# A chunked recurrence on one core: the two halves of a chunk taken one after the other, with four gaps for dense matmuls in place of three

## The chip, the cores and the metric

The kernel runs on one core of one Trainium2 chip. The metric is the device time of one execution in microseconds (us). PE is TensorE, PEld its weight loads, DVE VectorE, ACT ScalarE, POOL GpSimd, SP SyncE; DMAs are issued on SP's queue.

## The reference, cut to what matters

One layer runs (DEPTH is 1): RWKV-7 time mixing over 2048 tokens, 16 heads of 64 channels, width 1024. Projections give r, k, v, a gate and a decay for every token; then a state of 64x64 for each head is carried from token to token, and its output is normed by head, given a bonus, gated and projected out:

```python
def step(S, inp):
    r_t, w_t, k_t, v_t, kk_t, a_t = inp
    sa = jnp.einsum('bhvk,bhk->bhv', S, -kk_t)
    S = (S * w_t[:, :, None, :] + sa[..., None] * (kk_t * a_t)[:, :, None, :]
         + v_t[..., None] * k_t[:, :, None, :])
    return S, jnp.einsum('bhvk,bhk->bhv', S, r_t)
...
y = (y - mean) * lax.rsqrt(var + RW_GN_EPS)
y = y * gn_w + gn_b
y = y + jnp.sum(r_h * k_h * r_k, axis=-1, keepdims=True) * v_h
return (y * g) @ w_out          # and the layer adds x
```

## The kernel before, in words

**Stages.** The first stage projects v, the gate and the low-rank inputs for all tokens. The second makes k, r and, for every chunk of 32 tokens, the small matrices of the recurrence; its last part (function `last`, four steps for each of eight head groups) runs together with chunks 0 to 8. The third stage is the loop over chunks 9 to 63 with `chunk(ch, after)`. The change lies in `chunk` and in what goes with it, so in chunks 0 to 8, in the loop and in what follows it.

**A chunk.** 32 tokens, 16 heads. A chunk has two halves, w = 0 and w = 1, of four pairs of heads each. The work of one half, by the names of the code:

- `s_mm` (L255): 8 fp32 matmuls, into the bank `ybank` number w; each fp32 matmul is two instructions in the trace. `s_out` (L261): two ACT copies of 32x256.
- `u_mm` (L267): 8 matmuls of what `s_out` wrote, into `ubank`. `u_out` (L273): two ACT copies into `x`, the operand of the chunk.
- `y_mm` (L279): 8 matmuls, the chunk's output, into `ybank` number w. `y_out` (L290, L292): ACT copies to `y`, in every second chunk.
- `d_mm` (L300): 16 matmuls, the state, into the other half of the bank `ubank`. `d_out` (a DVE multiply, recorded at the helper's line L52 as x<-ubank,misc): two of 64x256 into the `x` of the next chunk.

Each matmul writes one strip of 32 of PE's columns. `s_mm`, `u_mm` and `y_mm` of a half use two of the four strips, `col(h, ch)` or `col(h, ch + w)`, which for neighbouring chunks are the other two; `d_mm` goes round all four.

**The order of the work.** All engines run their instructions in the order in which the code issues them. `chunk` issues three groups, each followed by a call `fill(i)`: `s_mm` of (ch, 0) interleaved with `u_mm` of (ch-1, 1); `u_mm` of (ch, 0) interleaved with `y_mm` of (ch-1, 1), then `d_mm` of (ch-1, 1); `d_mm` of (ch, 0), then `s_mm` of (ch, 1) interleaved with `y_mm` of (ch, 0). `finish` completes the last half. In the loop a `fill` is `after(i)`, which calls two planners:

- `background(us)` issues entries of the queues `evacs` (stores of the output) and `work`, each with a price in us written in the code, up to a budget; `served[1]` keeps what is left, but never more than one call's budget. An entry (None, None) ends a call, unless it is the first thing that the call meets. The first entry of a call is issued whatever its price.
- `fill(n)` issues about n output matmuls (L500) from the queue `dense`: 0.7 n when 36 or fewer wait (`LOW`), n when more, 1.3 n when over 72.

```python
served[1] = min(served[1] + us, us)
fresh = True
while evacs or work:
    u, fn = (evacs or work)[0]
    if not fresh and (u is None or u > served[1]):
        break
```

**The tail of 128 rows.** After chunks 12, 16, ..., 60, `work` gets `tail(t)`, the norm, bonus, gate and transposes of four finished chunks: squares on ACT, four sums and two seeds on DVE, three Newton steps on POOL, then five DVE operations for each of four parts, two groups of four transposes on PE (L460), a copy (L480) and a subtraction each; at its end 48 dense matmuls enter `dense`, whose two results make four `store` entries. After chunks 12, 16, ..., 40 up to ten entries of the inversion of the last two blocks' matrices follow (60 columns in all, two DVE operations each, price 0.5). `y` has three buffers: `more_y(t)` calls `background(1)` until the transposes of tail t-3 have been issued. When the loop is over, `tail(15)` is queued, and `background(2)` and `fill(6)` alternate until all queues are empty.

Of the kernel before, what the change touches and what calls it, by code (L numbers as in the profile page):

```python
# [10 lines left out]
I32 = mybir.dt.int32  # L11
# [12 lines left out]
NP = 8  # L24
# [1 line left out]
TB = 256  # L26
NC = TB // L
NORM_EPS = 1e-6
F, BG, EV, EV0, GWE, BNE, LOW, SLOW, FAST, INV, INVC = 4, (1.5, 1.3, 3.2), (0, 0, 0), (0, 0, 0), 0, 0, 36, 0.7, 1.3, (8, 10), 0.5
LIM = 1.0  # L30
TURN = 1e-9
INL = (0, 0, 3, 3, 3, 0, 0, 0)
# [8 lines left out]
def rwkv7_kernel(ctx, tc, a, T):  # L41
    nc = tc.nc
# [270 lines left out]
    def chunk(ch, fill):  # L313

        g, c = divmod(ch, NC)
        go = ch != first[0]
        if c == 2 and g + 1 < NB:
            load_g(g + 1)
        for p in range(4):
            s_mm(ch, 0, p)  # L320
            if go:
                u_mm(ch - 1, 1, p)
        s_out(ch, 0)
        if go:
            u_out(ch - 1, 1)
        fill(0)
        for p in range(4):
            u_mm(ch, 0, p)
            if go:
                y_mm(ch - 1, 1, p)  # L330
        if go:
            d_mm(ch - 1, 1)
        u_out(ch, 0)
        if go:
            y_out(ch - 1, 1)
            d_out(ch - 1, 1)
        if ch + 2 < NCH:
            load_v(ch + 2)
        if ch + 3 < NCH:
            load_c(ch + 3)  # L340
        fill(1)
        d_mm(ch, 0)
        for p in range(4):
            s_mm(ch, 1, p)
            y_mm(ch, 0, p)
        d_out(ch, 0)
        s_out(ch, 1)
        y_out(ch, 0)
        fill(2)

    def finish(ch):
        for p in range(4):
            u_mm(ch, 1, p)
        u_out(ch, 1)
        for p in range(4):
            y_mm(ch, 1, p)
        d_mm(ch, 1)
        d_out(ch, 1)
        y_out(ch, 1)

    dense, evacs, turned, served, al = deque(), deque(), set(), [0.0, 0.0], {}
    eng = lambda i: nc.gpsimd if i else nc.vector

    def fill(n):

        served[0] = min(served[0], 6) + n * (FAST if len(dense) > 2 * LOW else 1 if len(dense) > LOW else SLOW)
        while served[0] > 0 and dense:
            dense.popleft()[0]()
            served[0] -= 1
# [2 lines left out]
        while any(x[1] == key for x in dense):  # L372
            dense.popleft()[0]()

    def tail(t):

        y = ys.pop(t)
        b, q = t // 2, t % 2
        orow = slice(t * P, (t + 1) * P)
        bc = lambda z: z[:, :, None].broadcast_to([P, z.shape[1], N])  # L380
        bn = bns[b][:, 2 * q : 2 * q + 2]
        st, out = {}, []
        part = lambda c: (slice(None), c // 2, slice(4 * (c % 2), 4 * (c % 2) + 4))

        def step(us):
            return lambda fn: out.append((us, fn))

        def sml(nm):
            return al["sml"](f"{nm}{t}")

        def load_bonus(k):
            st["v", k] = v = al["v"](f"v{t}_{k}")
# [11 lines left out]
        @step(0.1)  # L404
        def _():
            st["var"], st["rst"] = sml("var"), sml("rst")
            load_bonus(0)
            load_bonus(1)
            square(0)
            square(1)  # L410

        for c in range(4):
            @step(0.4)
            def _(c=c):
                nc.vector.tensor_reduce(st["var"][part(c)], st["sq", c], AX.X, add)
                if c < 2:
                    square(c + 2)

        rs_tt = lambda o, x, y: al["rs"].tensor_tensor(out=o, in0=x, in1=y, op=mul)
# [1 line left out]

        @step(0.4)
        def _():
            var = st["var"]
            st["rg"], st["rm"] = sml("g"), sml("m")
            ts(var, var, 1.0 / N, GN_EPS, mul, add)
            ts(st["rg"].bitcast(I32), var.bitcast(I32), -0.5, 1597463007.0, mul, add)
            rs_ts(var, var, -0.5, mul)

        for it in range(3):  # L430
            @step(al["newton"])
            def _(it=it):
                var, g, m = st["var"], st["rg"], st["rm"]
                rs_tt(m, g, g)
                rs_tt(m, m, var)
                rs_ts(m, m, 1.5, add)
                rs_tt(g if it < 2 else st["rst"], m, g)

        for k in range(2):
            out.append((0.1, lambda k=k: scale_bonus(k)))  # L440
        out.extend([(None, None), (0.6, lambda: None)] * al["wait"])

# [64 lines left out]
            stt(x, st[n][:, q * 256 : q * 256 + 256], 0.5, x, mul, add)  # L507
            nc.sync.dma_start(a["out"][orow, o : o + 256], x)

        out.append((0.0, lambda: (load_gate(0), load_gate(1))))  # L510
        for k in range(2):
            for c in (2 * k, 2 * k + 1):
                out.append((0.7, lambda c=c: norm(c)))
                out.append((0.4, lambda c=c: bonus(c)))
                out.append((0.4, lambda c=c: shift(c)))
                out.append((0.4, lambda c=c: gating(c)))
            if k == 0:
                cut = len(out)
            if t == 0:

                out.append((TURN, lambda k=k: (transpose(k), high(k), rest(k))))
            else:
                out.extend([(None, None), (0, lambda k=k: (transpose(k), high(k))), (0.7, lambda k=k: rest(k))])
# [22 lines left out]
    with ExitStack() as p0:  # L546
# [152 lines left out]
        with ExitStack() as pb:  # L699
# [385 lines left out]
            with tc.manual_schedule(engines=MANUAL):  # L1085
# [107 lines left out]
                def fill_last(i):  # L1193
                    next(steps)
                    us = 0
                    while early:
                        if early[0][0] is None:
                            early.popleft()
                            if us:
                                break  # L1200
                        elif us + early[0][0] > LIM or early[0][0] is TURN and i != 2:

                            break
                        else:
                            us += early[0][0]
                            early.popleft()[1]()
                    if i == 2:
                        fill_last(3)

                steps = last()  # L1210
                for p in range(NP + 1):
                    chunk(p, fill_last)
                    if p == NP // 2:
# [6 lines left out]
                finish(NP)  # L1220
                while early:
                    fn = early.popleft()[1]
                    if fn:
# [2 lines left out]
    with ExitStack() as p1:  # L1226
# [44 lines left out]
        with tc.manual_schedule(engines=MANUAL):  # L1271
            work.extend((0.7, lambda q=q: wo_split(NP - 1, q)) for q in range(2))
            for x in tail(1):
                work.extend(x)
            z = c1.tile([P, L, L], F32, name="z_")
            tm = c1.tile([P, 4 * N], F32, name="tm_")
            inv = deque()
            for g in (NB - 2, NB - 1):
                load, *cols = inversion(g, z, lambda: tm)
                inv.extend([(0, load)] + [(None, None), (0, lambda: None)] * 4)  # L1280
                inv.extend((INVC, x) for x in cols)
            inv_g = inv[L + 6][1]

            inv_last = inv[-1][1]

            def after(i):
                background(BG[i])
                fill(F)

            for ch in range(NC + 1, NCH):  # L1290
                chunk(ch, after)
                if ch % 4 == 0 and ch > NC:
                    for x in tail(ch // 4 - 1):
                        work.extend(x)
                    for i in range(INV[1] if ch >= INV[0] else 0):
                        if inv:
                            work.append(inv.popleft())
                if ch == NCH - 2 * NC - 4:
                    assert len(inv) <= L - 1 and not any(x[1] is inv_g for x in work)
                if ch == NCH - NC - 4:  # L1300
                    assert not inv and not any(x[1] is inv_last for x in work)
            finish(NCH - 1)
            for x in tail(NCH // 4 - 1):
                work.extend(x)
            while work or dense or evacs:
                background(2)
                fill(6)
# [53 lines left out]
```

## Time and profile before

| | |
|---|---|
| time, median of 3 runs | 1640.67 us (1639.98 to 1648.12) |
| the profiled execution | 1649.95 us, its span 1648.1 us |
| busy in the span | PE 88%, PEld 72%, DVE 72%, ACT 46%, POOL 22% |
| chain that ended last | PE 50%, DVE 21%, ACT 9%, issue 6%, DMA 6% |
| mean granted TensorE clock | 0.972 |

The span goes from the first to the last instruction; 1.85 us of the profiled execution lie outside it. "Busy" counts a matmul until its modelled end, so a busy PE can still have gaps between its instructions. The shares are means over stages of different kinds; the chunk loop takes some 460 of the 1648 us.

### The profile page before, as it was taken

What the parts mean: (1) busy time and instruction counts of PE and PEld (TensorE: products, weight loads), DVE (VectorE), ACT (ScalarE), POOL (GpSimd) and SP (SyncE); (2) the same over time, 40 slices, a digit from 0 to 9 for tenths busy, and PEclk for the clock granted to TensorE, in tenths of its full rate; (3) what the DMA queues carried; (4) which work ended last, traced back from release to release, by engine and by line L of the source; (5) the groups of instructions that cost most, each with busy time, mean ns of one, the idle gap of its engine ahead of it and who ended that gap; (6) DMA issues with size and microseconds to landing.
All of it is one profiled execution on the core that took longest, in us unless ns stands there. A gap on an engine that the chain in (4) does not pass through costs nothing.

```text
span 1648.1 us, 48238 instructions
## 1 busy us (share of the span) xinstructions
PE 1442.2 (88%) x19024; PEld 1188.9 (72%) x19024; DVE 1187.9 (72%) x2876; ACT 762.3 (46%) x1908; POOL 358.8 (22%) x729
## 2 busy tenths in 40 slices
PE   3799999999989999999999998877777887787888
PEld 2578888888878888988888897765555555565556
DVE  7977687676835678888797978775567756785654
ACT  5653232233455545454545554665444444454440
POOL 4600000000002223232323223222222223222311
PEclk9899999999999999999999999998999999999999
DMA  5783333345563555666667677888555675566632
GB/s 180 231 260 138 129 134 122 112 144 167 197 192 84 154 114 147 133 162 154 157 163 152 163 154 189 220 239 210 162 164 175 174 185 173 163 183 184 194 114 74
DMA packets 413410, 269.79 MB, mean 164 GB/s; under 512 B 270048, under 2 KB 345440, under 8 KB 413184
## 3 DMA queue, kind: packets, MB, share of 16 engines
q1 hardware_dynamic: 411840, 262.19, 57.1%
q10 hardware_dynamic: 1344, 4.52, 1.2%
q8 instruction: 150, 2.46, 0.7%
q14 instruction: 76, 0.62, 0.1%
HBM read 159.26 MB, written 111.54 MB: 164 GB/s over the span
## 4 chain that ended last, share of the span: by engine, by line
PE 50%; DVE 21%; ACT 9%; issue 6%; DMA 6%; POOL 1%; SPq 1%; DVEq 0%; ACTq 0%; POOLq 0%
PE gps L582 9%; PE vps L582 8%; PE kps L582 7%; PE rps L890 5%; PE ops L500 4%; ACT x L273 4%; DVE x L52 3%; DVE y L52 3%; PE ubank L300 3%; PE lps L644 2%; PE ubank L267 2%; DVE z L52 2%; DVE tm L52 2%; PE mps L926 2%; ACT misc L261 2%
## 5 line engine op out<-in xcount | busy, mean ns | idle before, releaser
L52 DVE TENSOR_TENSOR x<-ubank,misc 64x256 f32<-64x256 f32 x216 | 91.2, 422 | 116.8 <-ACT x L273 100.2
L582 PE MATMUL kps<-mixbl,wkh 128*128 128x256 f32 x448 | 130.4, 291 | 15.2 <-DVE mixbl L187 15.2
L223 POOL MEMSET x<- 32x512 f32 x128 | 66.4, 519 | 329.1 <-PE ubank L300 249.8
L582 PE MATMUL kps<-mixbh,wkh 128*128 128x256 f32 x448 | 134.1, 299 | 0.2 <-DVE u L49 0.2
L890 PE MATMUL rps<-mixah,wrh 128*128 128x256 f32 x448 | 132.3, 295 | 2.1 <-ACT sq L61 2.1
L582 PE MATMUL kps<-mixbh,wkl 128*128 128x256 f32 x448 | 129.4, 289 | 0.0
L890 PE MATMUL rps<-mixal,wrh 128*128 128x256 f32 x448 | 126.5, 282 | 0.0
L890 PE MATMUL rps<-mixah,wrl 128*128 128x256 f32 x448 | 126.5, 282 | 0.0
L273 ACT COPY x<-ubank 32x256 f32<-32x256 f32 x220 | 79.9, 363 | 78.5 <-PE ubank L300 65.4
L500 PE MATMUL ops<-wol,oh 128*128 128x512 f32 x256 | 109.2, 426 | 1.8 <-issue 1.8
L500 PE MATMUL ops<-woh,oh 128*128 128x512 f32 x256 | 109.7, 429 | 0.4 <-DVE ol L52 0.4
L500 PE MATMUL ops<-woh,ol 128*128 128x512 f32 x256 | 109.7, 429 | 0.0
L300 PE MATMUL ubank<-x,dk 128*32 128x64 f32 x3456 | 72.7, 225 | 41.4 <-DVE x L52 18.6
L582 PE MATMUL vps<-wvh,mixah 128*128 128x512 f32 x256 | 104.0, 408 | 5.1 <-ACT mixah L97 4.7
L61 ACT ACTIVATE th<-wa,dprm 128x256 f32<-128x256 f32 x64 | 30.3, 474 | 163.4 <-PE wa L842 87.3
L300 PEld LDWEIGHTS ubank<-x,dk 128*32 128x32 f32 x3456 | 58.6, 113 | 63.8 <-ACT y L292 16.5
L582 PE MATMUL vps<-wvl,mixah 128*128 128x512 f32 x256 | 101.6, 398 | 0.0
L582 PEld LDWEIGHTS kps<-mixbl,wkh 128*128 128x128 f32 x448 | 88.8, 198 | 16.4 <-DVE mixbl L187 16.4
L582 PE MATMUL gps<-wgh,mixbh 128*128 128x512 f32 x256 | 99.7, 389 | 0.0
L582 PE MATMUL gps<-wgl,mixbh 128*128 128x512 f32 x256 | 99.7, 389 | 0.0
L582 PE MATMUL gps<-wgh,mixbl 128*128 128x512 f32 x256 | 99.6, 389 | 0.0
L582 PEld LDWEIGHTS kps<-mixbh,wkh 128*128 128x128 f32 x448 | 88.5, 198 | 9.1 <-issue 8.7
(335 smaller groups left out, 4400.8 us busy)
## 6 DMA issues: line engine op xcount, KB each, us to landing
stat<-sm_d SPq DMA_DIRECT2D x64, 512.0 KB, 4.7
dk<-bt_d SPq DMA_DIRECT2D x128, 128.0 KB, 4.1
sm_d<-ra SPq DMA_DIRECT2D x112, 128.0 KB, 2.5
sm_d<-mo SPq DMA_DIRECT2D x112, 128.0 KB, 2.6
bt_d<-bo SPq DMA_DIRECT2D x56, 256.0 KB, 2.7
up<-up_d SPq DMA_DIRECT2D x66, 128.0 KB, 2.5
xn<-x SPq DMA_DIRECT2D x32, 256.0 KB, 5.2
mkr_d<-mok SPq DMA_DIRECT2D x64, 128.0 KB, 1.7
```

The source lines that it names most:

```text
L52: return nc.vector.tensor_tensor(out=out, in0=in0, in1=in1, op=op)
L61: nc.scalar.activation(out, in_, f, **k)
L223: nc.gpsimd.memset(x[bu(h), h], 0.0)
L261: nc.scalar.copy(live(w, h)[bu(h)], bank[w][col(h, ch + w), 1])
L267: nc.tensor.matmul(bank[2][o, p], stat[ch % len(stat)][:, h, 4 * w + p, ca], live(w, h)[:, p], start=True, stop=True, tile_position=(0, o. ...
L273: (nc.vector.tensor_copy if w and h and evs[0] else nc.scalar.copy)(xs[ch % len(xs)][bu(h), h, 4 * w : 4 * w + 4], bank[2][col(h, ch)])
L300: nc.tensor.matmul(bank[3][o : o + L, p], d[:, h, 4 * w + p, o % 64 : o % 64 + L], x[:, h, 4 * w + p], start=True, stop=True, tile_positio ...
L500: nc.tensor.matmul(ps, l[:, ct], r(ct, ns), start=(ct == 0 and k == 0), stop=(ct == NCT - 1 and k == 2))
L582: nc.tensor.matmul(ps, x, y, start=first, stop=last)
L644: nc.tensor.matmul(lps, wls[i][x][:, ct], y[:, tok], start=(ct == 0 and i == 0 and k == 0), stop=(ct == NCT - 1 and i == 1 and k == 2))
L890: nc.tensor.matmul(ps, x, y, start=first, stop=last)
L926: nc.tensor.matmul(ps[H, c], bk[H, c], ra[H, c], start=True, stop=True, tile_position=(64 * h, 64 * h))
```

## The change

`chunk` takes one half after the other. Half w issues `s_mm` of (ch, w) alone; then, in the new function `end`, `d_mm`, `d_out`, `y_mm` and `y_out` of the half before it; then a fill; then `u_mm` of (ch, w) alone and a second fill. In the loop the four fills ask for 2, 4, 2, 4 dense matmuls in place of 4, 4, 4, and the budget of `background` is 1.3 us four times in place of 1.5, 1.3 and 3.2. In `tail`, the transposes are issued later among the DVE parts, and the first operation of a part has the price 0.8 in place of 0.7. From the end of chunk 56 `LOW` is 0. After chunk 62 the part of `tail(15)` for chunks 60 and 61 is queued, and the Newton steps go to DVE from there on; the rest is queued after the last chunk.

```diff
-F, BG, ..., LOW, SLOW, FAST, ... = 4, (1.5, 1.3, 3.2), ..., 36, 0.7, 1.3, ...
+F, BG, ..., LOW, SLOW, FAST, ... = (2, 4), 1.3, ..., 36, 0.7, 1.3, ...
...
+        for w in range(2):
+            for p in range(4):
+                s_mm(ch, w, p)
+            s_out(ch, w)
+            if w or go:
+                end(ch - 1 + w, 1 - w)
...
+            fill(2 * w)
+            for p in range(4):
+                u_mm(ch, w, p)
+            u_out(ch, w)
+            fill(2 * w + 1)
+
+    def end(ch, w):
+
+        d_mm(ch, w)
+        d_out(ch, w)
         for p in range(4):
...
+            y_mm(ch, w, p)
+        y_out(ch, w)
...
-        served[0] = min(served[0], 6) + n * (FAST if len(dense) > 2 * LOW else 1 if len(dense) > LOW else SLOW)
+        served[0] = min(served[0], 6) + n * (FAST if len(dense) > 2 * al["low"] else 1 if len(dense) > al["low"] else SLOW)
...
-    def tail(t):
+    def tail(t, ks=(0, 1)):
...
+        parts = [[(0.8, lambda c=c: norm(c)), (0.4, lambda c=c: bonus(c)), (0.4, lambda c=c: shift(c)), (0.4, lambda c=c: gating(c))]
+                 for c in range(4)]
+        if len(ks) == 1:
+            k = ks[0]
+            out.extend(parts[2 * k] + parts[2 * k + 1] + [(None, None), (0, lambda: (transpose(k), high(k))), (0.7, lambda: rest(k))])
...
+            turns = [[(None, None), (0, lambda k=k: (transpose(k), high(k)))] for k in range(2)]
+            rests = [[(0.7, lambda k=k: rest(k))] for k in range(2)]
+            out.extend(parts[0] + parts[1] + parts[2] + turns[0] + parts[3] + rests[0])
+            cut = len(out)
+            out.extend([(None, None), (0.0, lambda: None)] + turns[1] + rests[1])
...
-                    if i == 2:
-                        fill_last(3)
...
-                background(BG[i])
-                fill(F)
+                background(BG)
+                fill(F[i % 2])
...
+                if ch == NCH - 8:
+
+                    al["low"] = 0
+                if ch == NCH - 2:
+
+                    al.update(rs=nc.vector, newton=0.8, wait=0)
+                    work.extend(tail(NCH // 4 - 1, (0,))[0])
...
-            finish(NCH - 1)
-            for x in tail(NCH // 4 - 1):
-                work.extend(x)
+            end(NCH - 1, 1)
+            work.extend(tail(NCH // 4 - 1, (1,))[1])
```

## Rows read from the trace of the kernel before

**Rows 1.** Windows: chunks 0 to 8; the loop (length, busy PE to POOL, clock).

```profile
1030.00:1147.00 117.00, 89.93 (x2068) 76.17 (x2068) 81.56 (x195) 72.82 (x177) 23.31 (x51) 0.89 0.85 224
1147.00:1605.00 458.00, 361.19 (x9358) 258.56 (x9358) 303.01 (x767) 209.64 (x566) 124.32 (x313) 0.97 0.60 171
```

**Rows 2.** Timeline of PE: first instruction of chunk 10 and of chunk 63.

```profile
1147.09 0.34 PE L255 MATMUL ybank<-x,stat 128*32 128x64 f32 x3 [0.53 <-POOL m L419]
...
1597.70 0.25 PE L255 MATMUL ybank<-x,stat 128*32 128x64 f32 x2
```

**Rows 3.** Timeline of PE, one chunk of the loop (start, length, line, count, idle before).

```profile
1351.76 0.34 PE L255 MATMUL ybank<-x,stat 128*32 128x64 f32 x3 [0.23 <-issue]
...
1352.46 0.50 PE L500 MATMUL ops<-wol,oh 128*128 128x512 f32 x1
...
1354.16 0.25 PE L267 MATMUL ubank<-misc,stat 128*32 128x64 f32 x2 [0.51 <-ACT x L273]
...
1355.19 0.50 PE L500 MATMUL ops<-woh,ol 128*128 128x512 f32 x1
...
1357.20 0.31 PE L300 MATMUL ubank<-x,dk 128*32 128x64 f32 x7 [0.80 <-DVE x L52]
...
1358.42 0.50 PE L500 MATMUL ops<-woh,oh 128*128 128x512 f32 x1
...
1359.54 0.24 PE L255 MATMUL ybank<-x,stat 128*32 128x64 f32 x1
```

**Rows 4.** Timelines of ACT and DVE in the same chunk.

```profile
1355.42 0.75 ACT L273 COPY x<-ubank 32x256 f32<-32x256 f32 x2 [0.26 <-PE ubank L300]
...
1356.20 0.86 DVE L52 TENSOR_TENSOR x<-ubank,misc 64x256 f32<-64x256 f32 x2 [1.20 <-ACT x L273]
...
1358.08 0.88 DVE L52 TENSOR_TENSOR x<-ubank,misc 64x256 f32<-64x256 f32 x2
```

**Rows 5.** Timeline of PE in chunk 9, and the window that holds both (clock 0.50).

```profile
1140.72 1.07 PE L267 MATMUL ubank<-misc,stat 128*32 128x64 f32 x16
...
1143.72 1.08 PE L300 MATMUL ubank<-x,dk 128*32 128x64 f32 x32
1140.70:1144.60 3.90, 3.90 (x57) 2.87 (x60) 1.51 (x4) 1.70 (x5) 0.00 (x0) 0.50 0.91 210
```

**Rows 6.** Waits of PE from 1150 to 1600 us (total, times, longest).

```profile
PE yt L460 <- DVE y L52: 12.4, 17, 1.7
```

**Rows 7.** Timelines of ACT and DVE after the loop.

```profile
1606.61 0.37 ACT L292 COPY y<-ybank 128x256 f32<-128x256 f32 x1 [0.72 <-PE ybank L279]
...
1609.65 0.73 DVE L415 TENSOR_REDUCE var<-sq 128x4 f32<-128x256 f32 x2
1610.30 0.74 DVE L49 SCALAR_TENSOR_TENSOR xr<-ops,xr 128x256 f32<-128x256 f32 x2
...
1611.94 0.18 DVE L58 TENSOR_SCALAR g<-var 128x16 int32<-128x16 int32 x1
...
1623.98 0.69 DVE L52 TENSOR_TENSOR ol<-yt,oh 128x512 fp32r<-128x512 f32 x1 [1.28 <-ACT oh L480]
...
1626.83 0.42 DVE L52 TENSOR_TENSOR y<-y,rst 128x256 f32<-128x256 f32 x1
...
1628.66 0.42 DVE L52 TENSOR_TENSOR y<-y,gt 128x256 f32<-128x256 f32 x1
```

**Rows 8.** Chain that ended last, its last pieces (start, us, what).

```profile
1629.14 0.44 PE yt L460 x2
1629.58 14.80 PE ops L500 x65
```

**Rows 9.** Window with two of its dense matmuls: PE after it idled (clock is 0.50).

```profile
1622.90:1626.10 3.20, 3.20 (x9) 2.53 (x9) 1.95 (x5) 0.59 (x1) 0.00 (x0) 0.50 0.24 72
...
1624.40 0.63 PE L500 MATMUL ops<-woh,ol 128*128 128x512 f32 x1
1624.83 0.63 PE L500 MATMUL ops<-woh,oh 128*128 128x512 f32 x1
```

More of the change, by code (lines that the diff above doesn't have):

```diff
@@ L28 @@
 NORM_EPS = 1e-6
-F, BG, EV, EV0, GWE, BNE, LOW, SLOW, FAST, INV, INVC = 4, (1.5, 1.3, 3.2), (0, 0, 0), (0, 0, 0), 0, 0, 36, 0.7, 1.3, (8, 10), 0.5
+F, BG, EV, EV0, GWE, BNE, LOW, SLOW, FAST, INV, INVC = (2, 4), 1.3, (0, 0, 0), (0, 0, 0), 0, 0, 36, 0.7, 1.3, (8, 10), 0.5
 LIM = 1.0
@@ L318, in chunk @@
             load_g(g + 1)
-        for p in range(4):
[L320 to L361, printed above, removed]
+        for w in range(2):
[4 more added lines that the diff above has]
+                end(ch - 1 + w, 1 - w)
+            if w == 0:
+                if ch + 2 < NCH:
+                    load_v(ch + 2)
+                if ch + 3 < NCH:
+                    load_c(ch + 3)
+            fill(2 * w)
[6 more added lines that the diff above has]
+        d_out(ch, w)
+        for p in range(4):
+            y_mm(ch, w, p)
+        y_out(ch, w)
+    dense, evacs, turned, served, al, parts_of = deque(), deque(), set(), [0.0, 0.0], {"low": LOW}, {}
     eng = lambda i: nc.gpsimd if i else nc.vector
     def fill(n):
-        served[0] = min(served[0], 6) + n * (FAST if len(dense) > 2 * LOW else 1 if len(dense) > LOW else SLOW)
+        served[0] = min(served[0], 6) + n * (FAST if len(dense) > 2 * al["low"] else 1 if len(dense) > al["low"] else SLOW)
         while served[0] > 0 and dense:
@@ L373, in drain @@
             dense.popleft()[0]()
-    def tail(t):
-        y = ys.pop(t)
+    def tail(t, ks=(0, 1)):
+        y = ys[t]
+        if ks[-1]:
+            del ys[t]
         b, q = t // 2, t % 2
@@ L381, in tail @@
         bn = bns[b][:, 2 * q : 2 * q + 2]
-        st, out = {}, []
+        st, out = parts_of.setdefault(t, {}), []
+        cs, kk = range(2 * ks[0], 2 * ks[-1] + 2), slice(ks[0], ks[-1] + 1)
         part = lambda c: (slice(None), c // 2, slice(4 * (c % 2), 4 * (c % 2) + 4))
@@ L388, in sml @@
         def sml(nm):
-            return al["sml"](f"{nm}{t}")
+            return al["sml"](f"{nm}{t}_{ks[0]}")
         def load_bonus(k):
@@ L406, in _ @@
             st["var"], st["rst"] = sml("var"), sml("rst")
[L407 to L412, printed above, removed]
+            for k in ks:
+                load_bonus(k)
+            square(cs[0])
+            square(cs[1])
+        for c in cs:
             @step(0.4)
@@ L415, in _ @@
                 nc.vector.tensor_reduce(st["var"][part(c)], st["sq", c], AX.X, add)
-                if c < 2:
+                if c + 2 in cs:
                     square(c + 2)
@@ L423, in _ @@
         def _():
-            var = st["var"]
             st["rg"], st["rm"] = sml("g"), sml("m")
+            var, g = st["var"][:, kk], st["rg"][:, kk]
             ts(var, var, 1.0 / N, GN_EPS, mul, add)
-            ts(st["rg"].bitcast(I32), var.bitcast(I32), -0.5, 1597463007.0, mul, add)
+            ts(g.bitcast(I32), var.bitcast(I32), -0.5, 1597463007.0, mul, add)
             rs_ts(var, var, -0.5, mul)
@@ L432, in _ @@
             def _(it=it):
-                var, g, m = st["var"], st["rg"], st["rm"]
+                var, g, m, rst = (st[x][:, kk] for x in ("var", "rg", "rm", "rst"))
                 rs_tt(m, g, g)
@@ L436, in _ @@
                 rs_ts(m, m, 1.5, add)
-                rs_tt(g if it < 2 else st["rst"], m, g)
-        for k in range(2):
+                rs_tt(g if it < 2 else rst, m, g)
+        for k in ks:
             out.append((0.1, lambda k=k: scale_bonus(k)))
@@ L508, in store @@
             nc.sync.dma_start(a["out"][orow, o : o + 256], x)
[L510 to L516, printed above, removed]
-            if k == 0:
[L518 to L523, printed above, removed]
+        out.append((0.0, lambda: [load_gate(k) for k in ks]))
+        parts = [[(0.8, lambda c=c: norm(c)), (0.4, lambda c=c: bonus(c)), (0.4, lambda c=c: shift(c)), (0.4, lambda c=c: gating(c))]
[3 more added lines that the diff above has]
+            out.extend(parts[2 * k] + parts[2 * k + 1] + [(None, None), (0, lambda: (transpose(k), high(k))), (0.7, lambda: rest(k))])
+            if k == 0:
+                return out, []
+            cut = 0
+        elif t == 0:
+            turns = [[(TURN, lambda k=k: (transpose(k), high(k), rest(k)))] for k in range(2)]
+            cut = len(out)
+            out.extend(parts[0] + parts[1] + turns[0] + parts[2] + parts[3] + turns[1])
+        else:
+            turns = [[(None, None), (0, lambda k=k: (transpose(k), high(k)))] for k in range(2)]
+            rests = [[(0.7, lambda k=k: rest(k))] for k in range(2)]
+            out.extend(parts[0] + parts[1] + parts[2] + turns[0] + parts[3] + rests[0])
+            cut = len(out)
+            out.extend([(None, None), (0.0, lambda: None)] + turns[1] + rests[1])
         out.append((0.0, lambda: dense.extend((lambda n=n, ct=ct, k=k: mm(n, ct, k), t)
@@ L1219, in rwkv7_kernel @@
                             early.extend(x)
-                finish(NP)
+                end(NP, 1)
                 while early:
```

## The prediction, made blind

> **What bounds the kernel now.** I read the page first, then windows by stage, the timelines of PE, ACT and DVE over one chunk and over the end, and the waits. The loop has more than a quarter of the span, and PE is the busiest engine in it without being full: 361 of 458 us, at nearly full clock [rows 1]. From chunk 10 to chunk 63 a chunk takes (1597.70 - 1147.09) / 53 = 8.50 us [rows 2]. The chunk shown has no transposes and takes 7.78 us [rows 3]; the reader should see three gaps in front of its three groups: 0.23, 0.51 and 0.80, together 1.54. They are round trips. A group ends, ACT copies it out (0.75 for two copies), DVE multiplies it into the next operand (0.86), and PE goes on 0.14 us after DVE's end: 1357.06 to 1357.20 [rows 3, 4]. Four dense matmuls, 1.12 us from the first to the next group (1358.42 to 1359.54) [rows 3], are too short to cover two such copies in a row. What the mean has beyond this chunk is 0.72, of which 12.4 / 53 = 0.23 is PE waiting with transposes for DVE [rows 6].
>
> After the last `y_out` (1606.98) 41.1 us remain to the end of the span, 1648.1 [rows 7]: DVE finishes two tails, and from 1629.14 on PE works through transposes, 65 dense matmuls in 14.80 us (0.228 each), and 3.7 us of store and write [rows 8].
>
> **The groups that now run alone.** This is what the change costs on PE. In chunk 9, where `u_mm` has no partner, its 16 instructions take 1.07 us; the 32 of `d_mm`, three microseconds later at the same clock of 0.50, take 1.08 [rows 5]. Two strips hold PE as long as four. At full clock `u_mm`/`y_mm` and `d_mm`, 64 instructions, go from 1354.16 to the first dense matmul at 1355.19 [rows 3]: 1.03, or 0.44 each with 0.15 for the changeover. Before, a chunk had five such terms (three pairs and two `d_mm`); now it has eight. That is 3 x 0.44 = 1.3 us more per chunk, which the vanished gaps (1.54) must first pay for. Bounds: 0 if strips alone ran twice as fast, which [rows 5] speaks against, and 1.3.
>
> **A half chunk after.** I set `s_mm`'s start to 0. `d_mm` starts at 0.44, `y_mm` ends at 1.32, dense begins at 1.47. The loop's queue will hold fewer dense matmuls, about 11 a chunk, so 1.85 in the first gap and 3.65 in the second; with 1.12 for four and 0.23 for each one fewer, PE reaches `u_mm` at 1.47 + 0.63 = 2.10. But `u_mm` writes the bank that `d_out` reads. [Rows 4] show how such neighbours are kept apart: DVE's multiply at 1356.20 starts 0.03 after ACT's copy out of the other half of the same bank has ended, though the two share no column. So `u_mm` waits for `d_out`: from `d_mm`'s start to its `d_out`'s end went 1357.20 to 1358.96, 1.76 [rows 3, 4], plus 0.14, which puts `u_mm` at 0.44 + 1.90 = 2.34. DVE was there slightly late with other work; I take 2.25, with 2.10 and 2.34 as bounds. Then 0.44 + 0.15 and 1.04 of dense: a half takes 3.88, a chunk 7.76. `s_out` (0.44 + 0.2 + 0.75 = 1.4) and `u_out` (done 1.5 after `u_mm`'s start, wanted 2.1 after it) are covered by this; if DVE is late, nothing covers that: behind a held `u_mm` stand the dense matmuls and the whole next half, and ACT waits for it with `u_out`.
>
> The Trainium skill, PSUM — Partial Sum Buffer, section "PSUM bank collisions raise a hardware error", asks to guard PSUM by bank and quadrant and not by address. Its rule speaks against putting `d_out` right ahead of `u_mm`. By addresses `u_mm` would start at 2.10 and the forecast below would come to 1636 us; by the rule it is 1652. The trace agrees with the rule, in the 0.03 us just named.
>
> To 7.76 come the irregular losses. Of 0.72 the 0.23 of transposes goes, since these are now issued one part or more behind their inputs; of the other 0.49 I keep 0.35, since the copies have more cover than before (bounds 0 and 0.49).
>
> **The planner falls behind.** I counted the calls of `background` through, with the prices in the code. One tail takes 14 calls of 1.3, because each (None, None) ends a call and a part at 2.0 fills two; the two pairs of stores take two more. That is 16 calls for four chunks, all there are. The 60 inversion columns, two to a call, and the pauses after their loads take some 38 calls on top. About 28 are forced back by the three `y` buffers: 3, 4, 7, 6, 6, 1 and 1 calls in one place in chunks 37 to 61. In chunks 41 to 53 this puts the last DVE parts directly ahead of the transposes that need them; at 2.26 us a part (1626.83 to 1629.08) [rows 7], PE stands about 1.4 + 3.2 + 2.8 + 2.8 = 10 us, or 0.19 a chunk. So the loop's chunk is 7.76 + 0.35 + 0.19 = 8.30, and 54 chunks gain 54 x 0.20 = 11 us (bounds: 46 gained to 16 lost, from 7.65 and 8.80).
>
> The rest of the backlog lands behind the loop. When chunk 63 is issued, tail 13 has come to the middle of its third part, 14 has not begun, and the first half of 15, queued early, stands behind both. The same count of the kernel before has tail 14 in its last part there, and gives 65 dense matmuls after the last transposes, as [rows 8] show.
>
> **The end after.** DVE's remaining work in its order: 9 1/2 parts at 2.26 are 21.3; eight sums at 0.36 are 2.9; seeds and Newton steps, now on DVE, some 15 small operations at 0.2 for tail 14 and twice for 15, 9.0; six subtractions at 0.69, 4.1; six pairs of stores at 0.7, 4.2 [rows 7]. That is 41.5. About 1.5 of it runs before the last `y_out`. Three times DVE waits for transposes and their copy, 1.28 where nothing lies between [rows 7], and several times for results of dense matmuls: 5.7 in all, an estimate. Then 1.25 for the last transposes and copy, 48 x 0.228 = 10.9 [rows 8], and 3.7. After idling PE came back at half clock, 0.43 a dense matmul [rows 9]; for eight of them that adds 1.6. Sum 41.5 - 1.5 + 5.7 + 1.25 + 10.9 + 1.6 + 3.7 = 63, against 41.1: 22 us lost, though 17 dense matmuls no longer stand at the end (bounds: 15 with no waits and full clock, 28).
>
> **Chunks 0 to 8.** The extra PE time is at most 9 x 1.3 = 12 us, the gaps that may close at most 9 x 1.54 = 14. PE is busy 90 of 117 us [rows 1]. I take 0, with 6 either way. The loads are issued in the same place in the chunk, and the memsets on POOL and the DMAs on SP are the same ones: nothing.
>
> **Sum.** -11 + 22 + 0 = +11. The profiled execution (1649.95) would go to 1661. It lies 9.3 above the median of the runs, at the upper end of their spread, so I carry the difference to the median: 1640.67 + 11 = 1652.
>
> **Rivals.**
>
> *The loop sheds its waits.* `u_mm` is not held up (2.10) and the irregular losses vanish too: 2 x 3.73 + 0.19 = 7.65 a chunk, 46 us gained in the loop, 24 in all: 1617. For it: every copy but `d_out`'s has half a microsecond of slack. Against it: DVE is busy 303 of 458 us [rows 1], and one late operation of it stops PE. It is faster by over 0.5% from a chunk of 7.94 down. Chance 0.17.
>
> *Only addresses count, `u_mm` does not wait.* 2 x 3.73 + 0.35 + 0.19 = 8.00, 27 gained, 5 in all: 1636, no change. Against it stand [rows 4]. Chance 0.20.
>
> *DVE becomes the bound.* Two calls of 1.3 are about 2.9 us of real DVE work (a part priced 2.0 takes 2.26), and with 0.88 for `d_out` 3.8 of a half's 3.88. If lateness adds 0.25 a half, a chunk takes 8.80: 16 lost there, 1679 in all. Against it: many calls issue only pauses. Chance 0.13.
>
> My forecast has 0.50. About 0.5% (8 us) is what a measurement of this kernel can tell from no change. Faster: the first rival and a little of the second and of mine, 0.20; same: the second and the upper side of mine, 0.25; slower: 0.55. The range leaves out most of the first rival and half of the third: 1626 to 1678.
>
> **What would show it.** In the profile after: `u_mm` of 16 instructions holding PE as long as `d_mm` of 32; PE waiting for x L52 ahead of `u_mm` in most halves; a chunk of 8.0 to 8.6; parts of tails 13 and 14 behind the last chunk and some 60 us from the last `y_out` to the end. The prediction is wrong if alone groups take half the time, if the chunk falls below 7.9, or if the end takes under 50 us.

## The result, and the profile after

The changed kernel takes 1668.05 us (median of 4 runs, 1663.12 to 1675.05); the kernel before took 1643.52 beside it on the same chip. The ratio is 1.0138, with a 95% interval from 1.0094 to 1.0183: slower by some 24 us. The profiled execution took 1675.05, with a span of 1673.2.

Four rows of the timeline of ACT after split the span into stages: the first `s_out` of chunk 0, of chunk 9 and of chunk 63, and the last `y_out`.

```profile
1025.51 0.73 ACT L261 COPY misc<-yb 32x256 f32<-32x256 f32 x2 [5.68 <-PE yb L255]
...
1150.41 0.75 ACT L261 COPY misc<-ybank 32x256 f32<-32x256 f32 x2 [0.48 <-PE ybank L255]
...
1598.50 0.75 ACT L261 COPY misc<-ybank 32x256 f32<-32x256 f32 x2 [1.26 <-PE ybank L255]
...
1606.33 0.37 ACT L292 COPY y<-ybank 128x256 f32<-128x256 f32 x1 [1.17 <-PE ybank L279]
```

Chunks 0 to 8 take 1150.4 - 1025.5 = 124.9, the 54 chunks from the start of chunk 9 to that of chunk 63 take 448.1, and from the end of the last `y_out` (1606.7) to the end of the span there are 66.5. All profiles below are cut in this way, each by its own four rows (us; the last column is the median of the runs). The kernels were timed on several chips, on which the kernel before took 1643.5 to 1646.4. One execution each of e3, e5 and e11 ran slower at a lower granted clock (1709.84, 1692.70 and 1793.44 us) and is left out of the medians.

| kernel | chunks 0 to 8 | chunks 9 to 63 | per chunk | after the last `y_out` | median |
|---|---|---|---|---|---|
| before | 114.1 | 460.0 | 8.52 | 41.1 | 1643.52 |
| after | 124.9 | 448.1 | 8.30 | 66.5 | 1668.05 |
| e1_budget_18 | 123.2 | 481.9 | 8.93 | 37.6 | 1674.75 |
| e2_old_order_first_nine | 114.9 | 444.7 | 8.24 | 66.5 | 1661.23 |
| e3_pair_s_with_y | 127.0 | 435.3 | 8.06 | 66.7 | 1655.24 |
| e4_tail_edits_only | 114.8 | 439.3 | 8.14 | 66.1 | 1655.29 |
| e5_order_only | 124.3 | 469.1 | 8.69 | 39.2 | 1665.35 |
| e6_own_bank_for_d | 125.4 | 426.6 | 7.90 | 65.8 | 1648.31 |
| e7_two_dense_banks | 124.6 | 448.2 | 8.30 | 66.7 | 1672.80 |
| e8_old_order_tail_in_pace | 113.1 | 454.8 | 8.42 | 39.7 | 1636.85 |
| e9_old_order_d_bank | 115.3 | 435.5 | 8.07 | 40.2 | 1622.83 |
| e10_halves_all_mended | 113.3 | 442.1 | 8.19 | 36.0 | 1623.57 |
| e11_pair_all_mended | 114.3 | 436.9 | 8.09 | 36.5 | 1622.04 |
| e12_first_nine_d_bank | 118.7 | 443.4 | 8.21 | 67.2 | 1663.19 |

Three kernels have the same loop to the letter (after, e2, e12): 448.1, 444.7, 443.4. So a loop read from one profile scatters by about 5 us. Against the kernel before, the change costs 10.8 in chunks 0 to 8, saves 11.9 in the loop and costs 25.4 behind it: 24.3 in all.

Windows of both profiles (length, busy PE, PEld, DVE, ACT, POOL, then PE's clock), cut at these rows: the loop and the end, before and then after:

```profile
1138.41:1598.44 460.03, 363.06 (x9325) 259.95 (x9326) 301.50 (x765) 211.16 (x570) 124.67 (x314) 0.97 0.61 173
1606.98:1648.10 41.12, 32.98 (x142) 26.13 (x140) 18.62 (x43) 3.00 (x8) 5.14 (x15) 0.94 0.23 74
1150.41:1598.50 448.09, 415.29 (x9301) 304.46 (x9305) 288.32 (x732) 210.03 (x566) 121.61 (x301) 0.98 0.64 175
1606.70:1673.20 66.50, 46.96 (x188) 36.03 (x186) 38.07 (x119) 5.99 (x14) 1.04 (x1) 0.87 0.23 72
```

In the loop PE is busy 415.3 of 448 us where it was busy 363.1 of 460, although it does less: of the 768 dense matmuls of the output (`ops` in the trace) 588 start in this stretch, where 629 did. DVE does less there too (288.3 against 301.5) and is busy for 38.1 us behind the loop instead of 18.6. So a piece of the tails' work has moved from the loop to the end, DVE's operations and dense matmuls together.

One half chunk, PE's timeline after (`s_mm`; first dense matmul; `u_mm`; first dense matmul; the next `s_mm`):

```profile
1342.64 0.58 PE L255 MATMUL ybank<-x,stat 128*32 128x64 f32 x14
...
1344.04 0.50 PE L486 MATMUL ops<-woh,ol 128*128 128x512 f32 x1
...
1344.89 0.64 PE L267 MATMUL ubank<-aux,stat 128*32 128x64 f32 x16
1345.46 0.50 PE L486 MATMUL ops<-wol,oh 128*128 128x512 f32 x1
...
1346.58 0.59 PE L255 MATMUL ybank<-x,stat 128*32 128x64 f32 x14
```

and DVE's `d_out` in it:

```profile
1343.88 0.86 DVE L52 TENSOR_TENSOR x<-ubank,misc 64x256 f32<-64x256 f32 x2 [0.35 <-PE ubank L300]
```

`d_out` ends at 1344.74 and `u_mm` starts 0.15 later, at 2.25 of the half; the half takes 3.94.

Behind the loop, three of the pieces of the chain that ended last, 48 dense matmuls each:

```profile
1612.65 11.45 PE ops L486 x48
1631.51 13.58 PE ops L486 x48
1656.39 13.14 PE ops L486 x48
```

These are the results of tails 13, 14 and 15: three tails end behind the loop where two did. The 144 matmuls are 38.2 of the 66.5 us on this chain. Between them DVE does the tails one after the other (its timeline; the first row opens the sums of tail 14, the second is the last Newton step of tail 15's second half, the third the last `rest`):

```profile
1613.24 1.39 DVE L401 TENSOR_REDUCE var<-sq 128x4 f32<-128x256 f32 x4
...
1650.27 0.17 DVE L405 TENSOR_TENSOR rst<-m,g 128x8 f32<-128x8 f32 x1
...
1656.37 0.69 DVE L52 TENSOR_TENSOR ol<-yt,oh 128x512 fp32r<-128x512 f32 x1 [1.40 <-ACT oh L466]
```

### The profile page after: what moved, and what is told of

The parts are those of the page before. It is cut to its first block, busy times and chain, and to the rows that moved or that the text cites. A ratio compares the mean times of both kernels' runs of the same rounds, so it can differ in the third digit from the quotient of the medians.

```text
span 1673.2 us, 48351 instructions
## 1 busy us (share of the span) xinstructions
PE 1523.3 (91%) x19024; PEld 1257.4 (75%) x19024; DVE 1193.8 (71%) x2917; ACT 762.1 (46%) x1908; POOL 352.8 (21%) x703
## 5 line engine op out<-in xcount | busy, mean ns | idle before, releaser
L52 DVE TENSOR_TENSOR x<-ubank,misc 64x256 f32<-64x256 f32 x216 | 91.1, 422 | 125.2 <-PE ubank L300 121.9
L486 PE MATMUL ops<-woh,ol 128*128 128x512 f32 x256 | 113.3, 443 | 0.0
L883 PEld LDWEIGHTS rps<-mixah,wrh 128*128 128x128 f32 x448 | 85.9, 192 | 12.8 <-issue 8.6
L873 POOL TENSOR_TENSOR ra<-th,e 128x256 f32<-128x256 f32 x56 | 47.3, 844 | 218.5 <-issue 149.9
```

The source lines that it names most:

```text
L52: return nc.vector.tensor_tensor(out=out, in0=in0, in1=in1, op=op)
L486: nc.tensor.matmul(ps, l[:, ct], r(ct, ns), start=(ct == 0 and k == 0), stop=(ct == NCT - 1 and k == 2))
L873: (nc.vector if b == NB - 1 else nc.gpsimd).tensor_tensor(out=ra[:, :, ca], in0=c3(kn), in1=e[:, :, 0:L], op=mul)
L883: nc.tensor.matmul(ps, x, y, start=first, stop=last)
```

## The experiments

**More budget for DVE's planner.** The changed kernel with 1.8 instead of 1.3 a call:

```diff
-F, BG, EV, ... = (2, 4), 1.3, ...
+F, BG, EV, ... = (2, 4), 1.8, ...
```

> The changed kernel with the planner's budget at 1.8 us a call in place of 1.3, nothing else. Theory (the backlog is paid behind the loop): counted through, no call is forced any more and tail 15 has reached its seeds when the loop ends, so the end from the last y_out falls from 66.5 to about 40 us; the loop takes on some 20 us of DVE work and grows by 0 to 10. Time about 1647 us (1640 to 1655), against 1668. Rival (DVE already sets the loop): what leaves the end comes back as waits of u_mm for DVE in the loop, and the time stays within 1660 to 1672.

1674.75 us, ratio to before 1.0173 (1.0135 to 1.0211). The end fell as expected, by 28.9 to 37.6, but the loop grew by 33.8. My theory fell: the work is not hidden in the loop. The rival is nearer; the time is 3 us above its range. PE's waits from 1150 to 1575 us in this run (total, times, longest):

```profile
PE ubank L267 <- DVE x L52: 33.5, 34, 2.6
```

and in the changed kernel, over the same stretch:

```profile
PE ubank L267 <- DVE x L52: 15.1, 36, 1.3
PE yt L446 <- DVE y L52: 7.4, 5, 2.1
```

`u_mm` waits for `d_out` about as often, and each wait is more than twice as long, 18 us in all: `d_out` comes later on a DVE with more to do. The loop also got back 68 dense matmuls (656 against 588), at the 0.228 us of [rows 8] some 15 us of PE. Together the two are about what the loop lost.

**The old order in chunks 0 to 8 alone.**

```diff
                 for p in range(NP + 1):
-                    chunk(p, fill_last)
+                    chunk_old(p, fill_last)    # before's chunk, with its fill_last(3)
-                end(NP, 1)
+                finish(NP)
```

> The changed kernel with the order of before in chunks 0 to 8 alone. Theory (the new order costs there what it costs on PE, and finds no gaps to fill): s_mm of chunk 9 comes about 11 us earlier, 1149 to 1138, and the rest is as it was: about 1657 us (1653 to 1661). Rival (the loss there is a late load of the output weights and differs from run to run): 1664 to 1672.

1661.23, ratio 1.0108 (1.0065 to 1.0152). The nine chunks take 114.9, as before the change: the new order costs 10 us there.

**Pairing `s_mm` with `y_mm`.** `d_mm` first, then the two interleaved, so that two groups fewer run alone in a chunk:

```diff
+            e = (ch - 1 + w, 1 - w) if w or go else None
+            if e:
+                d_mm(*e)
+                d_out(*e)
             for p in range(4):
                 s_mm(ch, w, p)
+                if e:
+                    y_mm(*e, p)
             s_out(ch, w)
-            if w or go:
-                end(ch - 1 + w, 1 - w)
+            if e:
+                y_out(*e)
```

> The changed kernel with d_mm issued first in a half and then s_mm interleaved with the y_mm of the half before, which use the other two strips; u_mm stays alone. Theory (groups alone on two strips cost 0.44 us each, and u_mm waits for d_out): PE has 0.88 us less to do a chunk and d_out ends 0.44 earlier in a half, so a half falls from 3.9 to about 3.5 and a chunk by 0.7: 38 us in the loop, up to 8 before it, about 1625 us (1615 to 1640). Rival (DVE's lateness or the latency of the copies sets the chunk): less than 12 us, 1656 to 1668.

1655.24, ratio 1.0079 (1.0044 to 1.0114), close to the rival. The loop falls by 13 us to 8.06 a chunk, a third of what I expected: of the 0.88 us a chunk that the pairing was to give back, 0.24 came. PE's own busy time in the loop fell by 20.8 us (415.3 to 394.5), 0.39 a chunk, and 8 us of that became idle time. So pairing two groups saves less than 0.44 each, and the chunk is not set by PE's groups alone. In chunks 0 to 8 it gave nothing (127.0 against 124.9).

**The edits without the order.** Old order, old fills and budgets, with the changed tails and last rows:

```diff
-F, BG, EV, ... = (2, 4), 1.3, ...
+F, BG, EV, ... = 4, (1.5, 1.3, 3.2), ...
...
-        for w in range(2):                 # chunk of the change
+        for p in range(4):                 # chunk and finish of before
+            s_mm(ch, 0, p)
+            if go:
+                u_mm(ch - 1, 1, p)
...
-            end(NCH - 1, 1)
+            finish(NCH - 1)
```

> The kernel before with the edits of the tail, of the dense matmuls held back and of the last rows alone: the order of the chunk, the three fills of 4 and the budgets 1.5, 1.3 and 3.2 are those of before. Theory (the tail's later transposes and its price of 0.8 use up the calls, whatever the order of the chunk): counted through, tail 13 stands in its third part when the loop ends, here too, so the end takes 60 to 66 us; the loop gains up to 12 from the transposes' waits: 1654 to 1666 us. Rival (the smaller budget of the four calls starves the queue, and the old budgets keep up): the end takes 35 to 42 us and the time is 1632 to 1646.

1655.29, ratio 1.0064 (1.0041 to 1.0087). The end is 66.1, as the theory had it: the tail's edits make the backlog, whatever the order (e8 below traces it to the added (None, None) pauses and the price 0.8). The windows of the loop and the end:

```profile
1138.18:1577.48 439.30, 343.05 (x9276) 246.67 (x9277) 281.74 (x731) 208.91 (x564) 119.89 (x300) 0.98 0.63 177
1586.74:1652.80 66.06, 46.46 (x189) 35.62 (x187) 38.47 (x119) 5.99 (x14) 1.05 (x1) 0.87 0.23 74
```

Against the kernel before, 19.8 us of DVE's time have left the loop and 19.9 have come behind it, and 41 dense matmuls (588 against 629) have moved with them. The loop takes 8.14 a chunk, less than the 8.30 with the new order. So the loop of the changed kernel does not owe its gain to its order.

**The order without the edits.** The kernel before with the new `chunk`, fills of 2, 4, 2, 4 and four calls of 1.5, which sum to the old 6.0:

> The kernel before with the new order of the chunk alone (two halves, four fills of 2, 4, 2, 4), its old tails and the same 6.0 of planner budget a chunk (four calls of 1.5). Counted through, the planner has no backlog: chunk 63 leaves tail 14 in its third part, as before. Theory, formed after the run of the tail edits alone: the order itself is a loss, some 10 us in the first nine chunks and 0.17 a chunk in the loop, and what the changed kernel saved in its loop was DVE work put behind it. Then the loop takes 8.7 a chunk, the end about 43, and the kernel some 20 us more than before, 1665. Rival, the step of the prediction: the order itself takes 0.20 a chunk off the loop. Then the loop takes 8.3, and with 10 us lost in the first nine chunks the kernel takes about 1645, the time before.

1665.35, ratio 1.0127 (1.0103 to 1.0152), within 2 us of the theory in every stage but the end, which was 4 shorter. With the tails' work in it the new order's loop is slower than the old one's, 8.69 against 8.52. Its window, and PE's largest wait from 1150 to 1575 us:

```profile
1149.29:1618.40 469.11, 425.92 (x9361) 311.67 (x9364) 317.11 (x773) 213.80 (x574) 125.99 (x314) 0.99 0.62 172
...
PE ubank L267 <- DVE x L52: 29.7, 37, 2.3
```

**A bank of its own for `d_mm`.** The changed kernel with `d_mm`'s results in another PSUM bank in the loop, and, as its control, the changed kernel that only gives up the bank that this takes:

```diff
-    st[n] = sps.tile(..., tag="dense", bufs=3)
+    st[n] = sps.tile(..., tag="dense", bufs=2)       # all that the control changes
...
-        bank[2], bank[3] = ud[:, 0], ud[:, 1]
+        bank[2] = ud[:, 0]
+        bank[3] = sps.tile([P, 2, 4, N], F32, name="dbank")[:, 0]
```

> The changed kernel with d_mm's results in a PSUM bank of their own in the loop, paid for with one of the three banks of the dense matmuls (the next run has that alone). Theory: u_mm stands behind d_out because both use one bank; with two banks the halves in which u_mm waits for x L52 start it at about 2.1 instead of 2.25, the waits of u_mm for DVE vanish from the trace, and the loop is 0.1 to 0.3 a chunk (5 to 16 us) shorter than in the run with two dense banks alone. Rival: u_mm's hold is a matter of DVE's lateness and the half is set by the round of s, d, d_out and the next s; then u_mm starts earlier, the wait moves to s_mm, and the time stays within 4 us of that of the control.

> The changed kernel with two instead of three PSUM banks for the dense matmuls: the control for the run with d_mm's own bank. A row's second half of results then waits for its predecessor's stores. Expected: at most 10 us slower than the changed kernel, mostly behind the loop, where the stores are late; under the rival, that results leave in time, no difference.

The control takes 1672.80, ratio 1.0158 (1.0127 to 1.0188), and its loop 448.2: the missing dense bank costs nothing that shows. With `d_mm`'s own bank the kernel takes 1648.31, ratio 1.0018 (1.0002 to 1.0035), and the loop 426.6. That is 21.6 us in the loop and 24 in the medians, somewhat more than expected, for one address. The edit gives `d_mm` a tile of its own along with the bank; whether the program's waits go by the bank or by the tile was not separated. A half with the same two and four dense matmuls as the one shown above:

```profile
1331.12 0.58 PE L255 MATMUL ybank<-x,stat 128*32 128x64 f32 x14
...
1332.52 0.50 PE L486 MATMUL ops<-woh,ol 128*128 128x512 f32 x1
...
1333.18 0.64 PE L267 MATMUL ubank<-misc,stat 128*32 128x64 f32 x16
1333.75 0.50 PE L486 MATMUL ops<-wol,oh 128*128 128x512 f32 x1
...
1334.88 0.47 PE L255 MATMUL ybank<-x,stat 128*32 128x64 f32 x10
```

`u_mm` starts at 2.06 instead of 2.25, and the half takes 3.76 instead of 3.94. These halves are usual ones: over all from 1150 to 1575 us the median start of `u_mm` is 2.06 here and 2.26 in the changed kernel, where it comes within 0.2 us of the end of `d_out` in 89 of 104. PE's waits for x L52 ahead of `u_mm` are gone from the list.

**The edits in pace.** Old order and changed tails, but the norm at its old price and no added pauses:

```diff
-        parts = [[(0.8, lambda c=c: norm(c)), ...
+        parts = [[(0.7, lambda c=c: norm(c)), ...
-            turns = [[(None, None), (0, lambda k=k: (transpose(k), high(k)))] for k in range(2)]
+            turns = [[(0, lambda k=k: (transpose(k), high(k)))] for k in range(2)]
-            out.extend([(None, None), (0.0, lambda: None)] + turns[1] + rests[1])
+            out.extend([(None, None)] + turns[1] + rests[1])
```

> The old order of the chunk with the new tails (transposes issued a part after their inputs, the last rows' first chunks normed ahead, no dense matmuls kept back), but with the price of a norm at its old 0.7 and without the pauses added ahead of the transposes. Counted through, the planner then keeps pace: chunk 63 leaves tail 14 in its last part and 7 dense matmuls. Theory: pauses and price made the 66 us behind the loop, and the edits themselves help: the end falls to 36 to 39 (41 before), PE's waits with transposes go, and with a loop of 8.4 to 8.5 the kernel takes 1630 to 1640, faster than before. Rival: DVE work costs the loop as much as it costs behind it, and nothing is gained: 1640 to 1650.

1636.85, ratio 0.9942 (0.9925 to 0.9958): faster than before, by some 9.5 us. Where they come from can't be told from one profile each: the loop takes 454.8 against 460.0, about the scatter. The end takes 39.7, a little above what I expected. Against e4, which has the pauses and the price, the end is 26 us shorter and the loop 15.5 longer, with 650 dense matmuls in it instead of 588.

**The old order with `d_mm`'s bank.** The last kernel with the bank edit of above (`dense` with 2 buffers, `bank[3]` in the tile `dbank`) and nothing else:

> The old order with the tails in pace (the run before) and d_mm's own PSUM bank in the loop, two banks for the dense matmuls. Theory: in the old order dense matmuls stand between d_out and the next u_mm, so u_mm seldom waits for the bank, and DVE's lateness, which the bank does not change, sets the time; within 5 us of that run (1632 to 1642). Rival: the shared bank costs the old order as much as the new one, and the loop falls by some 0.3 a chunk: 1615 to 1625.

1622.83, ratio 0.9853 (0.9819 to 0.9886). My theory fell: the old order gains too, 14 us in the medians and 19 in the loop of these two profiles. It pays for the shared bank in another place. Before, `d_out` could not start until ACT had read `u_mm`'s results out of the bank [rows 4]. Here it starts while ACT's two copies, to 1352.13, still run (ACT and DVE):

```profile
1351.38 0.75 ACT L273 COPY x<-ubank 32x256 f32<-32x256 f32 x2 [0.80 <-PE ybank L279]
```

```profile
1351.86 0.86 DVE L52 TENSOR_TENSOR x<-dbank,misc 64x256 f32<-64x256 f32 x2 [4.92 <-PE dbank L300]
```

By the spacing of [rows 4] it would have started at 1352.16 with a shared bank, 0.30 us later. From 1150 to 1575 us, 38 of 104 `d_out` here start before these copies have ended, by 0.35 us on average ahead of that spacing, 13 us in all; with the shared bank (e8) none of 100 does, and 40 start 0.03 behind them.

**All of it together, with the new order in the loop.** Old order in chunks 0 to 8, own bank, tails in pace, four calls of 1.5; first with the new order, then also with the pairing. Beside the diffs of e2, e6 and e8, which it joins:

```diff
-F, BG, EV, ... = (2, 4), 1.3, ...
+F, BG, EV, ... = (2, 4), 1.5, ...
```

> All that the runs pointed to, with the new order in the loop: old order in chunks 0 to 8 (114 instead of 125), own bank for d_mm in the loop, tails in pace with four calls of 1.5 (counted through, chunk 63 leaves tail 14 pushed and 43 dense matmuls). Theory: DVE work costs the loop about what it costs behind it, so the 7.90 a chunk of the bank run rises by some 25 us / 54 = 0.45 to 8.3 or a little more, the end falls to 38 to 41, and the kernel takes 1632 to 1642, as the old order with the same tails. Rival: with the bank free, PE has room for the DVE work and the loop stays near 7.9: 1610 to 1620.

> As the last one, with d_mm put first and s_mm paired with y_mm in the loop, which took 0.24 a chunk off the changed kernel's loop. Theory: two groups a chunk less that hold PE alone; the pairing's gain stays, the loop is 0.15 to 0.3 a chunk (8 to 16 us) under the last run's and the kernel takes 1620 to 1632, below both kernels of the change and below the old order. Rival: with d_mm's own bank the pairing gives nothing more, since s_out then comes after d_mm and y_mm, and the time is that of the last run or longer.

1623.57, ratio 0.9864 (0.9835 to 0.9893), between theory and rival, and 1622.04, ratio 0.9852 (0.9819 to 0.9884). The loops of e6 and e10:

```profile
1144.78:1571.40 426.62, 409.61 (x9301) 302.08 (x9305) 290.29 (x731) 210.40 (x566) 121.98 (x301) 0.98 0.68 184
1133.05:1575.13 442.08, 427.53 (x9383) 314.24 (x9386) 315.19 (x775) 212.79 (x573) 127.91 (x316) 0.99 0.66 182
```

The returned work cost the loop 15.5 us (426.6 to 442.1), where 25 were expected. DVE is busy 24.9 us longer, but PE is too, by 17.9: 73 dense matmuls came back with DVE's work (661 against 588), some 17 us at 0.228. PE's idle time did not grow (17.0 and 14.6). So with the bank free the loop pays for PE's part, and DVE's seems to be hidden. The pairing gave 5 us in the loop, about the scatter, and nothing that shows in the medians. These two and e9 can't be told apart by their time: with the banks separate, the order of the chunk did not show in it.

**`d_mm`'s bank in chunks 0 to 8.** The changed kernel with `d_mm`'s results in the free half of a bank of phase A there:

```diff
-                bank[2], bank[3] = ud[:, 0], ud[:, 1]
+                bank[2], bank[3] = ud[:, 0], st["w1"][:, 1].rearrange("p (q n) -> p q n", n=N)
```

(`st["w1"]` is the tile `wa1`, widened to the whole bank and kept for the last eight groups.)

> The changed kernel with d_mm's results in another PSUM bank in chunks 0 to 8 alone: the unused half of the bank in which phase A sums its second small projection (it is written once a chunk there); the loop is as in the changed kernel. The first nine chunks took 114 before and 123 to 125 in the four runs with the new order. Theory: PE's gaps do not close there because u_mm waits for d_out behind DVE's work of phase A (17.7 us in 8 waits); with the bank apart the first nine chunks fall by 6 to 12, to 113 to 119, and the kernel to some 1658. Rival: the 11 us are the PE time of the groups that run alone (97.3 busy against 86.3) in a stage that PE's own work sets; then the first nine stay at 122 to 126 and the kernel at 1668.

1663.19, ratio 1.0098 (1.0061 to 1.0136). The nine chunks take 118.7: 6.2 of the 10.8 us went with the shared bank, 4.6 stayed. That is the upper end of the theory's range, so both were partly right. In the changed kernel, PE's largest wait from 1026 to 1150 us is

```profile
PE ud L267 <- DVE x L52: 17.7, 8, 7.5
```

and with the bank apart one wait of that size is left:

```profile
PE ud L267 <- ACT misc L261: 7.2, 1, 7.2
```

## Why the prediction was right, and where it was not

The direction was right, and the time fell in the range, 16 us above the value named; but the change cost 24 us where 11 were forecast. By terms, -11 + 22 + 0 was forecast and -11.9 + 25.4 + 10.8 measured. One term was mis-sized, chunks 0 to 8, and the loop's came out by luck: the new order cost 9 us there instead of gaining 11, and work that was put off hid it.

**Groups that run alone: right, a little too dear.** The 16 instructions of `u_mm` hold PE as long as forecast (1344.89 to 1345.46, 0.57 with the changeover). In e5, which has the new order and nearly the dense matmuls of before (635 against 629), PE is busy 62.9 us longer in the loop. Without those six matmuls that is 1.14 a chunk against 1.3, and the changeovers around a fourth gap are in it.

**A half chunk: right.** `u_mm` at 2.25 and a half of 3.88 were forecast; 2.25 and 3.94 were measured in a half without other waits.

**`u_mm` waits because of the bank: right.** The rival "only addresses count" priced a half without the hold at 3.73 and `u_mm` at 2.10; with banks apart 3.76 and 2.06 were measured, and its chunk of 8.00 came out as 7.90. What the prediction drew from the Trainium skill, PSUM — Partial Sum Buffer, section "PSUM bank collisions raise a hardware error" (guard PSUM by bank and quadrant, not by address), agrees with the waits of this program, and this pair of runs shows their price, 21.6 us. What would follow without such waits was not tried. That `d_out` of the kernel before paid for the bank too, on ACT's side, I had shown in [rows 4] and not followed up.

**The loop: right number by luck, reason wrong in part.** -11 was forecast, -11.9 measured. But the step "of the other 0.49 I keep 0.35, since the copies have more cover than before" failed. With the tails' work in it the new order loses 0.93 a chunk beyond the 7.76 (e5, 8.69), not 0.35: PE's waits for `d_out` ahead of a held `u_mm` are 29.7 us there, twice those of the changed kernel. What made the loop shorter is the work that the planner put off. The two halves of the change measured alone show it: the order adds 9 us to the loop (e5), the edits take 21 off it (e4) and add 25 behind it, and e8, which takes back only pauses and price, returns 15.5 of the 21. The put-off work is DVE's operations and the dense matmuls that follow from them; every run moved both, so what each alone is worth was not measured. The forecast had the backlog as a cost at the end only, and did not see that the same work leaves the loop. With it back in the loop, the rival "DVE becomes the bound" (8.80 a chunk) is nearer: 8.69 in e5 and 8.93 in e1. The term for late parts was about right: 10 us of waits with transposes were forecast, 7.4 measured.

**The end: right, 3 us short.** 63 was forecast, 66.5 measured, with DVE's work in the order counted. Until the last `rest` DVE's waits were 10.9 us, where 5.7 were allowed for, most of them for dense results, and one of those took 3.02. Its work was shorter than the sum had it, 38.1 against 40. Its waits from 1606.7 to 1657.06, and that one:

```profile
DVE xr L49 <- PE ops L486: 8.0, 5, 3.0
DVE ol L52 <- ACT oh L466: 2.9, 5, 1.4
...
1639.68 0.76 DVE L49 SCALAR_TENSOR_TENSOR xr<-ops,xr 128x256 f32<-128x256 f32 x2 [3.02 <-PE ops L486]
```

**Chunks 0 to 8: the mis-sized term.** "I take 0, with 6 either way" came out as +10.8. The step set 12 us of extra PE time against 14 us of gaps that may close. The extra time came. Between whole chunks, PE's windows have 97.33 busy of 125 after:

```profile
1025.00:1150.00 125.00, 97.33 (x2044) 84.18 (x2039) 80.92 (x203) 70.83 (x173) 23.64 (x51) 0.89 0.76 203
```

and 86.28 of 114 before:

```profile
1024.00:1138.00 114.00, 86.28 (x2037) 74.18 (x2031) 81.26 (x201) 71.28 (x173) 23.65 (x50) 0.90 0.84 229
```

That is 11 more, and PE stands idle for 27.7 in both: no gap closed. `u_mm`'s hold took their place, as e12 shows for 6 us of it. The hold was in the sum of a half chunk and should have been in this one too. Whether the last 4.6 are the alone groups' time was not tried by itself; e3, which pairs two of them, took no less there while the bank was shared.

**Not settled.** The three fastest kernels agree within 1.6 us, though PE is busy 363 of 436 us in the loop of e9, 428 of 442 in that of e10 and 417 of 437 in that of e11; what bounds each of them was not tested.

## What to carry to other kernels

When two engines take turns at one PSUM bank, separate their banks before changing the order of the work: one address gave 14 us here under the old order and 24 under the new, and with it neither order was better. When an edit delays work of a planner, count that work, with all that follows from it on other engines, in both places, where it leaves and where it lands; a loop that got shorter may only have postponed it. And before a reorder is costed, list which groups lose their partner on the other strips of PE, and use that cost in every stage that runs the code.

## What the runs showed that I had not expected

DVE's products of 128x256 in the tails usually take 0.42 us, but some take 0.9 to 1.3. In the run with `d_mm`'s own bank there are 14 of these from 1150 to 1575 us, and every one ran beside a multiply on POOL. On DVE:

```profile
1341.27 1.25 DVE L52 TENSOR_TENSOR y<-y,rst 128x256 f32<-128x256 f32 x1 [1.06 <-POOL rst L405]
1342.55 1.15 DVE L432 TENSOR_TENSOR y<-y,aux 128x256 f32<-128x256 f32 x1
1343.81 0.42 DVE L436 TENSOR_TENSOR y<-y,v 128x256 f32<-128x256 f32 x1
```

and POOL:

```profile
1341.19 2.23 POOL L384 TENSOR_TENSOR v<-v,misc 128x512 f32<-128x512 f32 x2
1343.48 1.09 POOL L223 MEMSET x<- 32x512 f32 x2
```

Two DVE products stretch over POOL's two multiplies; the third, beside POOL's memset, does not. The Trainium skill, SBUF — State Buffer, section "SBUF: two separate sides", has a rule that fits these rows: a DVE operation with two SBUF inputs and a GpSimd operation that reads SBUF exclude each other for a whole instruction.

After an idle stretch PE again came back at half clock, 0.43 us a dense matmul from 1632.10 on in the changed kernel; the window from 1631.50 has a granted clock of 0.50, that is 1.2 GHz:

```profile
1632.10 0.63 PE L486 MATMUL ops<-wol,oh 128*128 128x512 f32 x1
1632.53 0.63 PE L486 MATMUL ops<-woh,ol 128*128 128x512 f32 x1
...
1631.50:1636.30 4.80, 4.79 (x11) 3.76 (x12) 4.25 (x20) 0.58 (x2) 0.00 (x0) 0.50 0.17 54
```
